# Filter spectra stored side by side and read by one transfer, with the end of the convolution stage reordered

## The chip, the cores and the metric

The kernel runs on one core of a Trainium2 chip. The metric is the device time of one execution in microseconds (us); before the change it is 2328.96 us, the median of three runs (2328.45 to 2333.43). The engines are named as in the profile: PE is the matrix engine (PEld its weight loads), DVE the vector engine, ACT the scalar engine, POOL is GpSimd, and SP is the engine that issues nearly all DMA transfers, in the order of its queue. A transfer is carried by the core's 16 DMA engines, which are shared by all queues.

## What is computed

One encoder block on 2048 positions of 1024 channels in float32. The input projection feeds a Fourier group (512 channels) and a gated long convolution of order two (512 channels); both are normalised, joined, projected out and followed by an MLP.

```python
h   = RMSNorm(x);  p = h @ W_in            # Fourier | x1 | x2 | v
y_f = RMSNorm_f(Re(FFT2(Fourier group)))   # 8 groups of 64 channels
z   = short_conv(v)
for n, gate in enumerate((x1, x2)):        # circular convolution of length 4096 by FFT
    y = irfft(rfft(z, n=2 * l) * rfft(k[n]))[:, :l]
    z = gate * (y + z * long_d[n])
y_h = RMSNorm_h(z)
x   = x + concat(y_f, y_h) @ W_out
x   = x + relu(RMSNorm(x) @ W_fc1)**2 @ W_fc2
out = RMSNorm_final(x)
```

## The kernel before

The program has six stages: input projection, the Fourier transform of the Fourier group beside the making of the filters, the long convolution, the output projection (`project_out`), and the two MLP products (`fc1`, `fc2`). The change touches the second, the third and the start of the fourth.

**Filters** (`filters`, line 471). There are eight units, one for each of two orders `n` and four groups of 128 channels `ct`. A unit generates its filter (`generate`, which needs decay tables `dec` that SP loads for two steps at a time), transforms it in a first stage (`stage1`, eight steps `c`) and a second stage (`stage2`, line 569, eight steps `q` of four matmuls). ACT copies each step's result from PSUM to the tile `ks`, and after every second step SP stores 128 rows of 4 KB to the scratch tensor `kd[ct][n]` in DRAM, named `spec` in the profile. The tile is [128, 32 frequencies, 128 channels]: partitions 0 to 63 hold the real parts and 64 to 127 the imaginary ones.

**Long convolution** (`hyena`, line 630). There are again eight blocks, four channel groups for each of two orders. A block transforms its signal (`first`, eight steps; the results `pz` are transposed by DVE into `G`), and then in eight steps `q` of `second` (line 669) makes four matmuls `pz`, multiplies them with the spectrum, and passes the product `y` on. The spectrum must be in both partition halves: `ks[:, 0]` has the real parts in all 128 partitions and `ks[:, 1]` the imaginary ones. `spectrum` (line 647) therefore issues two transfers of 256 KB for each step, one to partitions 0 to 63 and one to 64 to 127, from the same DRAM rows in pieces of 2 KB. The tile `ks` has four buffers: the load of step q+4 waits until step q has used its own. ACT makes the exchanged copy `zs`, DVE makes `y = pz * ks[:, 0]`, POOL makes `zs * ks[:, 1]`, and the sum is POOL's or DVE's. Three steps later (`LAG = 3`) `inverse` transforms `y` back (matmuls `pv`, copied by ACT into `V`), `turn` transposes `V` to `W` on DVE, and `gate` makes the last matmuls (`pb`) and multiplies with the gate `xg` into `zz`. The blocks overlap: in block i's steps the turns of block i-1, the gates of block i-2 and the first stage of block i+1 are interleaved. Behind the loop the last block's three remaining inverse steps, its turns and its gates are written out.

**Start of the output projection.** `Out.weights` (line 762) loads 128 rows of `w_out` (tile `ost`, which takes a buffer of `ks`) and splits them into a high part on ACT and a low part on DVE (line 185), in buffers of `G` and `V`. `Out.ahead` (line 796) takes the first two token tiles ahead: it loads and normalises their Fourier rows (`yf`), transposes them (`pt_y`), and makes their 48 matmuls with the first half of `w_out` (`po`). In the program these stand behind the last block's gates. `project_out` then normalises the tiles' convolution rows from `zz` (`ssq_h`, `v_h`, `oyn`), transposes them and adds the second half's matmuls.

What sets the order: every engine runs its own queue in order. A scheduler emits the program's instructions into these queues by its own estimate of when each is ready, so a row can stand earlier than the text has it. Buffers of the same tag are handed on in the order of allocation.

Of the kernel before, what the change touches and what calls it, by code (L numbers as in the profile page):

```python
# [10 lines left out]
F32 = mybir.dt.float32  # L11
# [116 lines left out]
P = 128  # L128
# [6 lines left out]
def hybrid_block(ctx: ExitStack, tc: tile.TileContext, A, out):  # L135
    nc = tc.nc
# [334 lines left out]
    def filters(ctx, fp, gp, zp, zzs, norms, emb, wo, e1k, f2):  # L471
# [9 lines left out]
        p = pa("plongd")  # L481
# [3 lines left out]
        class Unit:  # L485
# [83 lines left out]
            def stage2(self, q):  # L569
                p = pa("pk2")  # L570
                for j in range(4):
                    nc.tensor.matmul(p[:, 128 * j : 128 * j + 128], lhsT=f2[:, 4 * q + j, :], rhs=self.G[:, :, 4 * q + j], start=True, stop=True)
                if q % 2 == 0:
                    self.ks = sp.tile([P, 8, 128], F32, tag="ks", name="ks", bufs=3)
                nc.scalar.copy(self.ks[:, 4 * (q % 2) : 4 * (q % 2) + 4, :], p.rearrange("p (f c) -> p f c", f=4))
                if q % 2:
                    nc.sync.dma_start(kd[self.ct][self.n][:, 4 * q - 4 : 4 * q + 4, :], self.ks)

# [50 lines left out]

    def hyena(hp, wp, rp, zz, e1, b1, f2, a2, out_weights, out_ahead):  # L630

# [5 lines left out]
        class Block:  # L637
            def __init__(self, n, ct):
                self.n, self.ct = n, ct
                self.cs = slice(128 * ct, 128 * ct + 128)  # L640
                self.y, self.ahead = {}, None

# [4 lines left out]
            def spectrum(self, q):  # L647

                ks = hp.tile([P, 2, 4, 128], F32, tag="ks", name="ks", bufs=4)
                src = kd[self.ct][self.n][:, 4 * q : 4 * q + 4, :].rearrange("(s p) f c -> p s f c", s=2)  # L650
                for hf in (slice(0, 64), slice(64, 128)):
                    nc.sync.dma_start(ks[hf], src)
# [16 lines left out]
            def second(self, q):  # L669
                ks = self.ahead if q == 0 and self.ahead else self.spectrum(q)  # L670
                p = pa("pz2")
# [8 lines left out]
                nc.gpsimd.tensor_mul(zs, zs, ks[:, 1])  # L680
                (nc.gpsimd if self is not blocks[7] and q in (0, 1, 2, 3) else nc.vector).tensor_add(y, y, zs)
                self.y[q] = y
# [31 lines left out]
        for i in range(8):  # L714
            cur, old, older, new = (blocks[j] if 0 <= j < 8 else None for j in (i, i - 1, i - 2, i + 1))
            for q in range(8):
                if new and q == 7:
                    new.ahead = new.spectrum(0)
                cur.second(q)
# [35 lines left out]

    class Out:


        def __init__(self, wp, zp, zz, gy):
            self.wp, self.zp, self.zz, self.gy, self.w, self.begun = wp, zp, zz, gy, [], {}  # L760

        def weights(self, hp, k):
            if k % 2 == 0:
                n = "G" if k < 4 else "V"
                self.pair = self.wp.tile([P, 32, 128], F32, tag=n, name=n, bufs=2).bitcast(FR).rearrange("p (n f) c -> p n (f c)", n=4)
            t = hp.tile([P, 2, 4, 128], F32, tag="ks", name="ost", bufs=4).rearrange("p s f c -> p (s f c)")
            nc.sync.dma_start(t, A["w_out"][128 * k : 128 * k + 128, :])
            hi, lo = (self.pair[:, 2 * (k % 2) + j, :] for j in range(2))
            split(hi, lo, t, self.gy[:, k : k + 1])
            self.w.append((hi, lo))  # L770
# [44 lines left out]
    def project_out(op, work, rp, b):  # L815
# [67 lines left out]
        for i in range(NT + 1):  # L883
# [17 lines left out]
            else:  # L901
# [9 lines left out]
                for n, tag in (("m5", "G"), ("m6", "G"), ("m3", "V"), ("m7", "V")):  # L911
                    t = work.wp.tile([P, 32, 128], F32, tag=tag, name=f"b{n}", bufs=2).bitcast(FR).rearrange("p (n f) c -> p n (f c)", n=8)
                    b[n] = t[:, 0:4], t[:, 4:8]
# [418 lines left out]
    with pool("raws") as rp:  # L1332
        with pool("wts") as wp:
            work = Out(wp, zp, zz, gy)
            with pool("hyena") as hp:
                hyena(hp, wp, rp, zz, e1z, b1, f2, a2, work.weights, work.ahead)
            tabs.close()
# [63 lines left out]
```

## Time and profile before

| | |
|---|---|
| median of 3 runs | 2328.96 us (2328.45 to 2333.43) |
| profiled execution | 2339.88 us, of it 2336.8 us from the first to the last instruction (the span) |
| mean granted PE clock | 0.986 |
| PE busy | 2250.9 us, 96% of the span |
| PE weight loads | 1860.4 us, 80% |
| DVE, ACT, POOL busy | 65%, 47%, 36% |
| DMA | 468.42 MB, mean 200 GB/s |
| spectra stored (`spec<-ks`) | 32 transfers of 512 KB, issued from 484.7 to 637.5 us |
| spectra loaded (`ks<-spec`) | 128 transfers of 256 KB, issued from 638.0 to 840.2 us |

All times inside the program are microseconds from the span's start. A busy share is the part of a stretch in which an engine worked; the "DMA share" is the mean busy share of the 16 DMA engines. KB are 1024 bytes, MB and GB are powers of ten. In the timeline a row has start, duration, engine, line, operation, out<-in, count, and in brackets the idle time before it with what ended it.

### The profile page before, as it was taken

The page shows a single profiled execution, that of the slowest core. Times are in us where ns is not written, and L with a number is a line of the kernel's source. Part 1 is how long each engine was busy: PE and PEld are TensorE (multiplying, and loading weights), DVE is VectorE, ACT ScalarE, POOL GpSimd, SP SyncE. Part 2 cuts the span into 40 slices and gives each one's busy share as a digit, 9 for nine tenths or more (in the row PEclk, how much of TensorE's full clock was granted, in tenths as well). Part 3 has the DMA queues.
Part 4 walks back from the last instruction along what each step waited for, and adds up shares of the span by engine and source line. Part 5 has one row for each costly group of instructions (what it writes and reads, how often), then busy time and mean ns, then how long its engine had stood idle before and what let it go on. Part 6 is the DMA issues. An engine that isn't in the chain of part 4 may idle for free. (4 is left out here: it accounts for less than half of the span.)

```text
span 2336.8 us, 31028 instructions
## 1 busy us (share of the span) xinstructions
PE 2250.9 (96%) x11025; PEld 1860.4 (80%) x11025; DVE 1514.5 (65%) x2248; ACT 1106.6 (47%) x1826; POOL 840.6 (36%) x633
## 2 busy tenths in 40 slices
PE   7999998999899979998999999999999999999998
PEld 6887787799787858886788877888888888888886
DVE  6998666677577774547544457444466666866667
ACT  6554211466455554544555556555543333533334
POOL 3345322567465522215755556555400000000000
PEclk9999999999999989999999999999999999999999
DMA  7535888457688986567544456444479666866631
GB/s 250 181 137 176 290 308 321 144 199 233 214 201 188 200 218 189 177 182 237 161 150 152 152 204 208 152 150 149 149 279 373 234 191 198 284 207 193 198 117 72
DMA packets 294780, 468.42 MB, mean 200 GB/s; under 512 B 18453, under 2 KB 142687, under 8 KB 290273
## 3 DMA queue, kind: packets, MB, share of 16 engines
q1 hardware_dynamic: 291265, 460.43, 61.9%
q10 hardware_dynamic: 3360, 6.02, 0.8%
q8 instruction: 86, 1.41, 0.3%
q14 instruction: 69, 0.57, 0.1%
HBM read 312.54 MB, written 152.27 MB: 199 GB/s over the span
## 5 line engine op out<-in xcount | busy, mean ns | idle before, releaser
L181 ACT CAST qahm<-ra 128x1024 fp32r<-128x1024 f32 x110 | 116.0, 1054 | 345.8 <-PE p2u L190 172.0
L182 DVE TENSOR_TENSOR qalm<-ra,qahm 128x1024 fp32r<-128x1024 f32 x110 | 134.7, 1224 | 154.8 <-ACT qahm L181 151.7
L1183 POOL TENSOR_TENSOR acc<-acc,gfin 128x512 f32<-128x512 f32 x4 | 5.1, 1278 | 632.9 <-DMA out<-acc 625.4
L189 PE MATMUL pu<-wh,xh 128*128 128x512 f32 x512 | 206.4, 404 | 5.8 <-ACT wh L184 4.8
L190 PE MATMUL pu<-wl,xh 128*128 128x512 f32 x512 | 203.3, 397 | 5.9 <-DVE wl L182 3.7
L191 PE MATMUL pu<-wh,xl 128*128 128x512 f32 x512 | 203.2, 397 | 5.7 <-DVE xl L182 5.7
L190 PE MATMUL p2u<-qblm,qahm 128*128 128x512 f32 x504 | 196.2, 389 | 0.3 <-DVE qblm L182 0.3
L189 PE MATMUL p2u<-qbhm,qahm 128*128 128x512 f32 x504 | 195.9, 389 | 0.0
L191 PE MATMUL p2u<-qbhm,qalm 128*128 128x512 f32 x504 | 195.8, 389 | 0.0
L397 POOL TENSOR_TENSOR acc<-acc,cw 128x512 f32<-128x512 f32 x45 | 60.9, 1353 | 206.1 <-DVE acc L374 204.8
L182 DVE TENSOR_TENSOR qblm<-rb,qbhm 128x1024 fp32r<-128x1024 f32 x110 | 134.0, 1219 | 1.1 <-ACT qbhm L181 1.1
L181 ACT CAST ahm<-s 128x512 fp32r<-128x512 f32 x124 | 76.7, 621 | 94.0 <-PE p1v L190 54.1
L190 PEld LDWEIGHTS pu<-wl,xh 128*128 128x128 f32 x512 | 98.3, 192 | 28.7 <-DVE wl L182 4.1
L191 PEld LDWEIGHTS pu<-wh,xl 128*128 128x128 f32 x512 | 98.2, 192 | 28.3 <-DVE xl L182 7.7
L189 PEld LDWEIGHTS pu<-wh,xh 128*128 128x128 f32 x512 | 98.0, 192 | 27.8 <-ACT wh L184 6.2
L182 POOL TENSOR_TENSOR alm<-W,ahm 128x512 fp32r<-128x512 f32 x63 | 85.5, 1358 | 91.4 <-ACT ahm L181 91.4
L181 ACT CAST qbhm<-rb 128x1024 fp32r<-128x1024 f32 x110 | 115.3, 1048 | 4.6 <-DMA a1m<-c 2.8
L190 PEld LDWEIGHTS p2u<-qblm,qahm 128*128 128x128 f32 x504 | 94.6, 188 | 20.3 <-DVE qblm L182 0.8
L189 PEld LDWEIGHTS p2u<-qbhm,qahm 128*128 128x128 f32 x504 | 94.6, 188 | 20.2 <-issue 0.3
L191 PEld LDWEIGHTS p2u<-qbhm,qalm 128*128 128x128 f32 x504 | 94.6, 188 | 19.6
L181 ACT CAST ahm<-W 128x512 fp32r<-128x512 f32 x94 | 57.6, 615 | 103.4 <-PE p1u L190 100.8
L191 PE MATMUL p1u<-bm,alm 128*128 128x512 f32 x252 | 99.9, 396 | 6.4 <-DVE alm L182 6.4
(387 smaller groups left out, 6456.8 us busy)
## 6 DMA issues: line engine op xcount, KB each, us to landing
W<-in_w_fc SPq DMA_DIRECT2D x66, 512.0 KB, 4.6
ks<-spec SPq DMA_DIRECT2D x128, 256.0 KB, 6.8
rb<-td SPq DMA_DIRECT2D x64, 512.0 KB, 4.1
ra<-a1m SPq DMA_DIRECT2D x56, 512.0 KB, 6.0
ra<-a0m SPq DMA_DIRECT2D x54, 512.0 KB, 10.7
rb<-in_w_fc SPq DMA_DIRECT2D x46, 512.0 KB, 4.5
f<-in_w_fc SPq DMA_DIRECT2D x16, 1024.0 KB
td<-f SPq DMA_DIRECT2D x16, 1024.0 KB, 4.7
```

The source lines that it names most:

```text
L181: nc.scalar.copy(hi, src)
L182: (eng or nc.vector).tensor_sub(lo, src, hi)
L189: nc.tensor.matmul(o, lhsT=lh, rhs=rh, start=start, stop=False, skip_group_check=more)
L190: nc.tensor.matmul(o, lhsT=lh, rhs=rl, start=False, stop=False, skip_group_check=more)
L191: nc.tensor.matmul(o, lhsT=ll, rhs=rh, start=False, stop=stop, skip_group_check=more)
L397: nc.gpsimd.tensor_add(m1, m1, cw[:, 3, :])
L1183: nc.gpsimd.tensor_mul(acc[i][:, c], acc[i][:, c], gfin[:, c])
```

## The change

Three things are changed.

First, the spectrum's layout in DRAM is [64 partitions, 8 steps, 2 halves, 512] in place of [128, 32, 128], so that the real and the imaginary part of a step lie side by side. Each step of `stage2` has its own tile and stores it alone: 256 KB, whose DRAM side is walked half by half (2 x 64 rows of 2 KB). A step of `spectrum` is one load of 512 KB: its DRAM side is the same 64 rows of 4 KB taken twice (a leading dimension of 2 with stride 0), its SBUF side 128 partitions.

Second, in the last block the spectra of steps 2 to 7 are loaded at step 1; four of them go to a tile in `W`'s buffer. The loads of the first two token tiles' Fourier rows and of the first four pieces of `w_out` are issued at step 5, and the block's own gate load at step 6. Two of the block's sums move from DVE to POOL.

Third, the splits of the first four pieces of `w_out` and the 48 Fourier matmuls `po` stand ahead of the last block's turns and gates, and the buffers of the four pairs of pieces are G, V, G, V in place of G, G, V, V.

```diff
-    kd = [[scratch(f"spec{i}{n}", [P, 32, 128]) for n in range(2)] for i in range(4)]
+    kd = [[scratch(f"spec{i}{n}", [64, 8, 2, 512]) for n in range(2)] for i in range(4)]
...
-                if q % 2 == 0:
-                    self.ks = sp.tile([P, 8, 128], F32, tag="ks", name="ks", bufs=3)
-                nc.scalar.copy(self.ks[:, 4 * (q % 2) : 4 * (q % 2) + 4, :], p.rearrange("p (f c) -> p f c", f=4))
-                if q % 2:
-                    nc.sync.dma_start(kd[self.ct][self.n][:, 4 * q - 4 : 4 * q + 4, :], self.ks)
+                ks = sp.tile([P, 512], F32, tag="ks", name="ks", bufs=6)
+                nc.scalar.copy(ks, p)
+                nc.sync.dma_start(kd[self.ct][self.n].rearrange("p q s x -> s p q x")[:, :, q], ks)
...
-                ks = hp.tile([P, 2, 4, 128], F32, tag="ks", name="ks", bufs=4)
-                src = kd[self.ct][self.n][:, 4 * q : 4 * q + 4, :].rearrange("(s p) f c -> p s f c", s=2)
-                for hf in (slice(0, 64), slice(64, 128)):
-                    nc.sync.dma_start(ks[hf], src)
+                if self is blocks[7] and q > 3:
+                    if q == 4:
+                        self.room = rp.tile([P, 4, 2, 4, 128], F32, tag="W", name="ks4")
+                    ks = self.room[:, q - 4]
+                else:
+                    ks = hp.tile([P, 2, 4, 128], F32, tag="ks", name="ks", bufs=4)
+                src = kd[self.ct][self.n][:, q].rearrange("p s x -> p (s x)")
+                nc.sync.dma_start(ks.rearrange("p s f c -> p (s f c)"), src.unsqueeze(0).broadcast_to([2, 64, 1024]))
...
-                (nc.gpsimd if self is not blocks[7] and q in (0, 1, 2, 3) else nc.vector).tensor_add(y, y, zs)
+                (nc.gpsimd if q in ((0, 1) if self is blocks[7] else (0, 1, 2, 3)) else nc.vector).tensor_add(y, y, zs)
...
+                if i == 7:
+                    if q == 1:
+                        cur.ahead.update((k, cur.spectrum(k)) for k in range(2, 8))
+                    elif q == 5:
+                        ahead = work.ahead(hp)
+                        next(ahead)
+                        for k in range(4):
+                            work.load(hp, k)
+                    elif q == 6:
+                        cur.load()
...
-        old.load()
         for q in range(8 - LAG, 8):
             old.inverse(q)
-        ahead = out_ahead(hp)
-        next(ahead)
+        for k in range(0, 2):
+            work.weights(hp, k)
         for q in range(4):
             older.gate(q)
-            old.turn(2 * q)
-            old.turn(2 * q + 1)
+        for k in range(2, 4):
+            work.weights(hp, k)
+        next(ahead)
+        for c in range(8):
+            old.turn(c)
         next(ahead, None)
-        for k in range(0, 4):
-            out_weights(hp, k)
         for q in range(4):
             old.gate(q)
-        next(ahead, None)
         for k in range(4, 8):
-            out_weights(hp, k)
+            work.weights(hp, k)
```

The first place is SP's queue where the last two units' spectra are stored and the first block's loaded (`spec_65`, `spec_67` and so on are the tensors of single units; the sizes are those of the written side). Before:

```order
222 L577 DMA spec_63<-ks 128x1024 x2
223 L170 DMA a_5695<-in_a 128x4096
224 L577 DMA spec_63<-ks 128x1024
225 L170 DMA b_5697<-in_b 128x128
226 L577 DMA spec_65<-ks 128x1024 x4
227 L577 DMA spec_67<-ks 128x1024 x4
228 L652 DMA ks<-spec_60 64x2x512 x14
```

After:

```order
224 L576 DMA spec_63<-ks 2x64x512 x3
225 L171 DMA a_5759<-in_a 128x4096
226 L576 DMA spec_63<-ks 2x64x512 x2
227 L171 DMA b_5761<-in_b 128x128
228 L576 DMA spec_65<-ks 2x64x512 x8
229 L576 DMA spec_67<-ks 2x64x512 x8
230 L656 DMA ks<-spec_60 128x1x1024 x4
231 L644 DMA xg<-gates_58 128x16x128
```

There are twice as many stores of half the size, written as 2 x 64 rows, and half as many loads of twice the size; the stores still stand ahead of the first load in the same queue.

The second place is DVE's queue from the last block's last sum `y<-y,zs` to the norm of the first convolution rows (`v_h`). Before, from the end of the turns:

```order
956 L703 TENSOR_TENSOR zz<-pb,xg 128x4x128
957 L203 TENSOR_SCALAR nw_s<-nw_s,rc_s 128x1
958 L418 STREAM_TRANSPOSE W<-V 128x8x2x32 x2
959 L185 SCALAR_TENSOR_TENSOR G<-ost,gy,G 128x1024
960 L182 TENSOR_TENSOR yl<-pt_y,yh 128x512
961 L185 SCALAR_TENSOR_TENSOR G<-ost,gy,G 128x1024
962 L182 TENSOR_TENSOR yl<-pt_y,yh 128x512
963 L185 SCALAR_TENSOR_TENSOR G<-ost,gy,G 128x1024 x2
964 L703 TENSOR_TENSOR zz<-pb,xg 128x4x128 x4
965 L185 SCALAR_TENSOR_TENSOR V<-ost,gy,V 128x1024 x4
966 L216 TENSOR_SCALAR v_h<-ssq_h 128x1 x2
```

After:

```order
960 L685 TENSOR_TENSOR y<-y,zs 128x512
961 L186 SCALAR_TENSOR_TENSOR G<-ost,gy,G 128x1024 x2
962 L707 TENSOR_TENSOR zz<-pb,xg 128x4x128 x2
963 L186 SCALAR_TENSOR_TENSOR V<-ost,gy,V 128x1024
964 L707 TENSOR_TENSOR zz<-pb,xg 128x4x128 x2
965 L186 SCALAR_TENSOR_TENSOR V<-ost,gy,V 128x1024
966 L183 TENSOR_TENSOR yl<-pt_y,yh 128x512 x2
967 L419 STREAM_TRANSPOSE W<-V 128x8x2x32 x8
968 L186 SCALAR_TENSOR_TENSOR G<-ost,gy,G 128x1024 x2
969 L186 SCALAR_TENSOR_TENSOR V<-ost,gy,V 128x1024 x2
970 L707 TENSOR_TENSOR zz<-pb,xg 128x4x128 x4
971 L217 TENSOR_SCALAR v_h<-ssq_h 128x1 x2
```

The eight turns now stand behind four splits and the two `yl`, and all eight splits stand ahead of the last gates, where four stood behind them.

The third place is PE's queue at the same point. Before:

```order
2201 L673 MATMUL pz_7484<-G,f_2594 128x128 x4
2202 L689 MATMUL pv<-y,a_5695 128x128 x16
2203 L702 MATMUL pb<-G,b_5697 64x512 x8
2204 L785 MATMUL pt_y<-ident,yf 128x128 x4
2205 L785 MATMUL pt_y<-turn,yf 128x128 x4
2206 L702 MATMUL pb<-W,b_5697 64x512 x8
2207 L189 MATMUL po<-G,yh 128x512
```

After:

```order
2201 L677 MATMUL pz_7525<-G,f_2594 128x128 x4
2202 L693 MATMUL pv<-y,a_5759 128x128 x16
2203 L706 MATMUL pb<-G,b_5761 64x512 x8
2204 L803 MATMUL pt_y<-ident,yf 128x128 x4
2205 L803 MATMUL pt_y<-turn,yf 128x128 x4
2206 L190 MATMUL po<-G,yh 128x512
```

The 48 matmuls `po` start right behind the transposes, and the last gates `pb<-W` come behind them.

More of the change, by code (lines that the diff above doesn't have):

```diff
@@ L627, in filters, with hyena @@
                     units[j // 2].scale(2 * (j % 2) + 1, nc.vector)
-    def hyena(hp, wp, rp, zz, e1, b1, f2, a2, out_weights, out_ahead):
+    def hyena(hp, wp, rp, zz, e1, b1, f2, a2, work):
         def big(nm):
@@ L640, in __init__ @@
                 self.cs = slice(128 * ct, 128 * ct + 128)
-                self.y, self.ahead = {}, None
+                self.y, self.ahead = {}, {}
             def load(self):
@@ L669, in second @@
             def second(self, q):
-                ks = self.ahead if q == 0 and self.ahead else self.spectrum(q)
+                ks = self.ahead.pop(q) if q in self.ahead else self.spectrum(q)
                 p = pa("pz2")
@@ L717, in hyena @@
                 if new and q == 7:
-                    new.ahead = new.spectrum(0)
+                    new.ahead[0] = new.spectrum(0)
                 cur.second(q)
@@ L760, in __init__, with load @@
             self.wp, self.zp, self.zz, self.gy, self.w, self.begun = wp, zp, zz, gy, [], {}
+            self.raw = {}
+        def load(self, hp, k):
+            self.raw[k] = hp.tile([P, 2, 4, 128], F32, tag="ks", name="ost", bufs=4).rearrange("p s f c -> p (s f c)")
+            nc.sync.dma_start(self.raw[k], A["w_out"][128 * k : 128 * k + 128, :])
         def weights(self, hp, k):
+            if k not in self.raw:
+                self.load(hp, k)
             if k % 2 == 0:
-                n = "G" if k < 4 else "V"
+                n = "GVGV"[k // 2]
                 self.pair = self.wp.tile([P, 32, 128], F32, tag=n, name=n, bufs=2).bitcast(FR).rearrange("p (n f) c -> p n (f c)", n=4)
-            t = hp.tile([P, 2, 4, 128], F32, tag="ks", name="ost", bufs=4).rearrange("p s f c -> p (s f c)")
-            nc.sync.dma_start(t, A["w_out"][128 * k : 128 * k + 128, :])
             hi, lo = (self.pair[:, 2 * (k % 2) + j, :] for j in range(2))
-            split(hi, lo, t, self.gy[:, k : k + 1])
+            split(hi, lo, self.raw[k], self.gy[:, k : k + 1])
             self.w.append((hi, lo))
@@ L910, in project_out @@
                     split(*ahead[n], src)
-                for n, tag in (("m5", "G"), ("m6", "G"), ("m3", "V"), ("m7", "V")):
+                for n, tag in (("m5", "G"), ("m6", "V"), ("m3", "G"), ("m7", "V")):
                     t = work.wp.tile([P, 32, 128], F32, tag=tag, name=f"b{n}", bufs=2).bitcast(FR).rearrange("p (n f) c -> p n (f c)", n=8)
@@ L1335, in hybrid_block @@
             with pool("hyena") as hp:
-                hyena(hp, wp, rp, zz, e1z, b1, f2, a2, work.weights, work.ahead)
+                hyena(hp, wp, rp, zz, e1z, b1, f2, a2, work)
             tabs.close()
```

## The prediction

> **What bounds the kernel now.** I read the page first, then the busy times by stretch, the waits and the DMA issues of the two stretches in which spectra are stored and loaded, and last the timeline from the last spectrum to the first output matmuls.
>
> ```profile
> span 2336.8 us, 31028 instructions
> PE 2250.9 (96%) x11025; PEld 1860.4 (80%) x11025; DVE 1514.5 (65%) x2248; ACT 1106.6 (47%) x1826; POOL 840.6 (36%) x633
> ```
>
> Over the whole span PE is the bound: 86 us of 2336.8 are not matmul time. No edit here takes matmuls away, so a gain can only come out of that idle time. A loss has no such limit. The change rebuilds transfers, so the question is what the DMA engines do in the stretches that hold them.
>
> ```profile
> L577 SPq DMA_DIRECT2D spec<-ks x32: 319/320/1562, 484.7 to 637.5; - x32
> L652 SPq DMA_DIRECT2D ks<-spec x128: 573/605/4610, 638.0 to 840.2; - x128
> ```
>
> These are the issues of the two transfers on SP's queue, with count, issue durations in ns, and the time of the first and the last. I cut the program there: 484.7 to 641.2 us (stores), 641.2 to 850.3 us (loads, until the last one has landed), and 850.3 to 883.0 us (up to the first `po` of the convolution half). The last two rows below are stretches elsewhere with DMA at its limit.
>
> ```profile
> core 0: us, PE busy (x) PEld busy (x) DVE busy (x) ACT busy (x) POOL busy (x), PEclk, DMA share, GB/s
> 484.70:641.20 156.50, 146.93 (x1067) 133.46 (x1066) 106.84 (x185) 85.51 (x172) 99.82 (x83) 0.98 0.65 218
> 641.20:850.30 209.10, 193.54 (x1346) 168.39 (x1346) 154.28 (x239) 114.66 (x198) 120.35 (x107) 0.98 0.89 200
> 850.30:883.00 32.70, 26.95 (x109) 16.11 (x108) 24.68 (x49) 19.07 (x33) 5.24 (x5) 0.81 0.78 229
> 856.00:858.00 2.00, 2.00 (x12) 0.68 (x10) 1.70 (x3) 0.00 (x0) 0.00 (x0) 1.00 1.02 408
> 1740.00:1760.00 20.00, 20.00 (x90) 16.57 (x89) 16.18 (x16) 10.15 (x10) 0.00 (x0) 1.00 1.04 393
> ```
>
> Read the last two columns together. Between 641.2 and 850.3 us the 16 DMA engines are busy for 0.89 of the time, yet they move 200 GB/s: 200 / (16 x 0.89) = 14.0 GB/s per busy engine. In the two limit rows an engine moves 408 / 16 = 25.5 and 393 / 16 = 24.6 GB/s. So the half-partition loads, most of this stretch, are slow for each engine. There are 64 spectrum steps (eight blocks by eight), so a step takes 209.1 / 64 = 3.3 us, with 193.54 / 64 = 3.0 us of matmuls in it: DMA and PE are nearly level. What PE waits for there:
>
> ```profile
> engine line waited for: us in total, times, longest us
> PE pv L689 <- DVE y L681: 14.6, 14, 3.8
> ```
>
> The product `y` comes late because its spectrum does. 14.6 us is nearly all that faster loads could win there (15.6 us are idle).
>
> **How many engines carry a transfer.** This decides the case. Both new transfers have a DRAM side whose outermost dimension is 2: the store walks 2 halves by 64 rows of 2 KB, the load takes the same 64 rows of 4 KB twice. All old ones start with 64 or 128 rows. The page shows that this dimension can matter, in ACT's queue (packets, MB, share of 16 engines) and in the list of ACT's DMA issues:
>
> ```profile
> q10 hardware_dynamic: 3360, 6.02, 0.8%
> ...
> a1m<-c ACTq DMA_DIRECT2D x8, 256.0 KB, 2.3
> a1m<-s ACTq DMA_DIRECT2D x6, 256.0 KB, 4.8
> nb<-full ACTq DMA_DIRECT2D x6, 128.0 KB, 2.3
> nb<-full ACTq DMA_DIRECT2D x6, 126.0 KB
> out<-acc ACTq DMA_DIRECT2D x2, 256.0 KB
> a0m<-es ACTq DMA_DIRECT2D x1, 256.0 KB
> ```
>
> 17 transfers of 128 rows, 6 of 64 and 6 of 63 rows, each row 2 KB, are 2176 + 384 + 378 = 2938 packets, and 2938 x 2 KB is the 6.02 MB of the row. The other 422 packets carry next to no bytes; I read them as one closing packet for each engine of each transfer. With 16 engines always, 29 x 16 = 464 would be there. 422 is 23 x 16 + 6 x 9: the 63-row transfers ran on 9 engines, and 9 is the largest number up to 16 that divides 63. So a transfer is cut along its outermost dimension into equal parts, one for each engine. By the same reading an outermost 2 gives **two engines** to every new store and load. No transfer of before has so small an outer dimension, so this is an extrapolation; its other end is all 16 engines, rival A. I take the two engines, since the 63-row transfers are the only ones here whose row count 16 doesn't divide, and they follow it.
>
> The Trainium skill says the same in a rule that speaks against this change: in "DMA: Bandwidth & Descriptors", section "Why a DMA increments its semaphore by 16 and not by 1", the number of engines is the largest one up to 16 that divides the slowest dimension other than 1 of both sides, and the section "Rules for kernel authors" names a leading zero-stride broadcast of c copies as confined to at most c engines. By this rule the sum below stands; without it, rival A's would. The trace agrees for 63 rows (9 engines) and shows nothing for 2.
>
> **The sum.** The traffic of the two stretches and landing times (median us from issue), first the stores' stretch, then the loads':
>
> ```profile
> DMA packets 16216, 34.12 MB, mean 218 GB/s; under 512 B 942, under 2 KB 9262, under 8 KB 16075
> ...
> dec<-in_decay SPq DMA_DIRECT2D x20, 512.0 KB, 4.0
> spec<-ks SPq DMA_DIRECT2D x32, 512.0 KB, 3.7
> ```
>
> ```profile
> DMA packets 34614, 41.79 MB, mean 200 GB/s; under 512 B 2158, under 2 KB 18368, under 8 KB 34595
> ...
> ks<-spec SPq DMA_DIRECT2D x124, 256.0 KB, 6.9
> ```
>
> - Stores: 64 of 262,144 B by two engines at 24.6 GB/s each: 16.8 MB / 49.2 GB/s = 341 us.
> - Loads: 64 of 524,288 B at 25.5 GB/s each: 33.6 MB / 51 GB/s = 658 us, 10.3 us a step where it takes 3.3 now. Four buffers keep the queue full, so the two engines never run dry while PE waits. Matmuls (3.0 us a step) and everything of DVE and POOL lie beside it.
> - All other transfers of the two stretches still use 16 engines, the two busy ones among them, behind whatever is queued there: 34.12 + 41.79 - 16.8 - 33.6 = 25.5 MB, 1.6 MB for each engine, 63 us at 25.5 GB/s and 114 us at 14.0. I take 80, nearer to the first, since these are mostly whole-partition transfers.
> - Added waits: stores are issued twice as often, and the `dec` loads stand behind them in SP's queue. A `dec` load lands in 4.0 us now; behind six queued stores (six buffers, 5.3 us each) its part on the two engines comes some 30 us later. PE, ACT and DVE wait for the filter that it feeds. Mostly the two engines go on working meanwhile; where the stores are drained before the next filter is made they stand idle, once a unit for about one old landing, 4.0 us in five units: 20 us. Bounds: nothing, and 80.
>
> Together 341 + 658 + 80 + 20 = 1099 us in place of 156.5 + 209.1 = 365.6: **+733 us**.
>
> The rate has bounds too. Below 14.0 GB/s per busy engine nothing ran in these rows, above 25.5 nothing either. The 14.0 stems from 16 engines all writing into one partition half at a time; two engines do not get in each other's way there, so I take the limit rows' rate. The other end is rival C.
>
> **The tail (edits two and three).** Rows from the timeline (start, duration, engine, line, operation), and group rows of DVE from 640 to 890 us (count | busy us, mean ns):
>
> ```profile
> 851.62 0.69 DVE L681 TENSOR_TENSOR y<-y,zs 128x512 f32<-128x512 f32 x1 [0.65 <-POOL zs L680]
> ...
> 864.67 6.08 PE L702 MATMUL pb<-W,b 128*64 128x512 f32 x16
> ...
> 869.79 2.48 DVE L703 TENSOR_TENSOR zz<-pb,xg 128x512 f32<-128x512 f32 x4
> ...
> 870.68 0.50 PE L189 MATMUL po<-G,yh 128*128 128x512 f32 x1
> ...
> 872.19 3.75 DVE L185 SCALAR_TENSOR_TENSOR V<-ost,gy,V 128x1024 fp32r<-128x1024 f32 x3
> ...
> 877.56 0.21 DVE L216 TENSOR_SCALAR v_h<-ssq_h 128x1 f32<-128x1 f32 x2
> ...
> 881.48 0.39 PE L191 MATMUL po<-G,yl 128*128 128x512 f32 x1
> ...
> 882.98 0.50 PE L189 MATMUL po<-V,oyh 128*128 128x512 f32 x1 [0.24 <-ACT oyh L181]
> ```
>
> ```profile
> L703 DVE TENSOR_TENSOR zz<-pb,xg 128x512 f32<-128x512 f32 x32 | 21.8, 689 | 8.9 <-PE pb L702 8.9
> L185 DVE SCALAR_TENSOR_TENSOR G<-ost,gy,G 128x1024 fp32r<-128x1024 f32 x4 | 5.0, 1269 | 0.0
> L418 DVE STREAM_TRANSPOSE W<-V 128x512 f32<-128x512 f32 x56 | 36.1, 680 | 9.3 <-ACT V L690 9.1
> L182 DVE TENSOR_TENSOR yl<-pt_y,yh 128x512 fp32r<-128x512 f32 x2 | 1.4, 685 | 0.0
> ```
>
> The 48 `po` (870.68 to 881.87, 11 us of PE) move ahead of the gates `pb` and then lie beside DVE's turns; behind the gates only the norm is left. DVE becomes the chain. From the end of its last `y` (852.31) the new order gives it four splits (4 x 1.27 = 5.1), four `zz` (2.8), two `yl` (1.4), eight turns (5.4), four splits (5.1) and four `zz` (2.5): 22.3 us. From `v_h` to the first `po` on `oyh` it is 882.98 - 877.56 = 5.4 us as before. So the first convolution `po` is at 852.3 + 27.7 = 880.0 in place of 883.0: **-3 us**. What hides the loads of `w_out` and of `yf` here is that they are issued three steps earlier; if they come late, up to 3 us of this are lost. The two sums moved to DVE's neighbour and the removed buffer exchanges lie beside waits for spectra, so I cost them at nothing. Behind 883 us the program is the same.
>
> **Result of the sum.** The profiled execution took 2339.88 us: 2339.9 + 733 - 3 = 3070. It lies 10.9 us above the median of 2328.96, so the forecast is 3070 - 11 = 3059, said as **3060 us**.
>
> **The rivals.**
>
> *A, not slower: all 16 engines carry the new transfers.* Then the load fills 128 partitions at once. The limit rows, both of whole-partition transfers, give 408 GB/s against 200: a 512 KB load would take 1.3 us, below the 3.0 us of matmuls. Most of the 14.6 us of waits go, and the last block's `y` comes earlier; I keep 9 of them, because the turns of `G` and the POOL products stay, and 3 us of the tail: 2317 us. It decides as soon as a step's load lands within 3 us. For it speaks the 14.0 against 25.5 GB/s; against it the count of closing packets. Should the loads stay as slow as now on 16 engines, only the tail counts: 2326, within 0.2%, which is about what a measurement of this kernel can tell from no change.
>
> The Trainium skill's "SBUF — State Buffer", section "Door 1: The DMA port swizzle (why `[64,N]` ≈ `[32,N]`)", says that 64 partitions reach only half of the memory's ports. The trace agrees with its 14.0 GB/s per engine; by this rule alone the time would be rival A's.
>
> *B, only one of the two is confined.* Both have the 2 on the DRAM side only, the load as a reading side with stride 0 and the store as a writing side; one of them may be cut along the partitions instead. Loads alone: 658 + 30 of others - 209 = +479, less 3: 2805. Stores alone: 341 + 50 + 20 - 156.5 = +254, less rival A's 12: 2571.
>
> *C, two engines at the low rate.* At 14.0 GB/s each the loads take 33.6 MB / 28 GB/s = 1200 us, 542 more: 3600.
>
> **How the numbers follow.** Forecast 0.78; A 0.16 (0.13 faster, 0.03 within 0.2%); B 0.02 for each half; C 0.02. The forecast's own range is 2960 to 3380: downward no idle engines (-20), the others at 63 (-17) and a rate a tenth above the limit rows (-65 on the loads); upward a load rate half-way between 14.0 and 25.5 (+193), the others at 114 (+34) and 80 us of idle engines (+60), with some 30 for PE's clock in the waits. It holds most of its 0.78; to leave out no more than 2 in 10 the range takes in the loads-alone case and becomes **2780 to 3380**; A, the stores-alone case and C stay outside. Faster 0.13, same 0.03, slower 0.84.
>
> **What would show it.** Two engines: a `ks<-spec` load lands 30 to 41 us after its issue (three or four queued at 10.3) in place of 6.9; a store in tens of us in place of 3.7; the stretches' DMA share is below 0.25 and the rate near 50 to 70 GB/s; PE's waits become `pv` for `y` in nearly every step, some 7 us each, with the same matmul time. The tail: `po` before `pb<-W`, and some 28 us from the last `y` to the first `po` on `oyh`. The forecast is wrong if loads land within 10 us, if the DMA share in the loads' stretch stays above 0.5, or if one of the two stretches keeps its length.

## The result and the profile after

The changed kernel takes 3048.72 us (median of 4 runs, 3047.74 to 3052.54) against 2330.1 us before: ratio 1.3084, 95% interval 1.3053 to 1.3115. The forecast was 3060 us.

First the head of the page of the changed kernel, with the busy time of each engine:

```profile
span 3046.8 us, 31011 instructions
PE 2372.3 (78%) x11025; PEld 1953.1 (64%) x11025; DVE 1510.7 (50%) x2246; ACT 1106.2 (36%) x1826; POOL 842.7 (28%) x635
```

The work is the same, the matmuls number 11025 as before. The span has grown by 710 us, PE's busy time by only 121 (its mean granted clock is 0.883 in place of 0.986); the rest is time in which PE does nothing. Next the issues of the two new transfers (count, shortest, median and longest issue in ns, first and last time), and the stretches of the stores, of the loads, and of the tail, followed by two short stretches in which next to nothing but stores (810 us) or loads (1515 us) run:

```profile
L576 SPq DMA_DIRECT2D spec<-ks x64: 477/4786/11240, 477.3 to 848.4; - x64
L656 SPq DMA_DIRECT2D ks<-spec x64: 482/5743/21542, 853.5 to 1523.1; - x64
```

```profile
core 0: us, PE busy (x) PEld busy (x) DVE busy (x) ACT busy (x) POOL busy (x), PEclk, DMA share, GB/s
477.30:853.50 376.20, 204.66 (x1142) 176.37 (x1140) 104.40 (x191) 86.47 (x173) 100.51 (x84) 0.75 0.26 89
853.50:1559.80 706.30, 263.54 (x1284) 219.89 (x1284) 154.93 (x240) 120.41 (x209) 122.53 (x109) 0.66 0.19 64
1559.80:1587.00 27.20, 23.22 (x96) 13.94 (x96) 22.92 (x31) 9.57 (x13) 1.27 (x1) 0.87 0.25 84
...
810.00:840.00 30.00, 12.48 (x25) 7.08 (x25) 4.30 (x6) 3.52 (x6) 0.00 (x0) 0.50 0.13 51
1515.00:1535.00 20.00, 5.85 (x24) 5.26 (x24) 2.59 (x4) 3.50 (x5) 1.27 (x1) 0.59 0.13 52
```

The stores' stretch went from 156.5 to 376.2 us, the loads' from 209.1 to 706.3. In the short stretches the DMA share is 0.13, which is 2 engines of 16 (0.125), and they move 51 and 52 GB/s: 25.5 and 26 GB/s for each of two engines, what the limit rows of before had for each of sixteen. SP's issue of one transfer takes 4.8 and 5.7 us at the median where 0.3 and 0.6 us were enough before: I read this as a full queue at the two engines, with SP standing in the issue itself. What DVE waits for in the loads' stretch (853 to 1535 us; total, times, longest):

```profile
DVE y L683 <- DMA ks<-spec: 291.8, 40, 13.8
```

In 40 of the 61 steps of this stretch the product waits for its spectrum, 7.3 us each time. In the chain of work that ended last, transfers `ks<-spec` make up 74.6% of the time from 870 to 1560 us. In the stores' stretch (477 to 853 us) the filters wait for their `dec` loads, which stand behind the stores in SP's queue, as the prediction had it:

```profile
DVE kt L509 <- DMA dec<-in_decay: 148.0, 12, 17.3
```

One more row counts the engines directly. It is that of SP's queue (packets, MB, share of 16 engines), of the kernel before

```profile
q1 hardware_dynamic: 291265, 460.43, 61.9%
```

and of the changed kernel:

```profile
q1 hardware_dynamic: 284865, 460.42, 45.0%
```

Nearly the same bytes, 6400 packets fewer. Before, the stores had 32 x 128 rows of 4 KB and the loads 128 x 64 x 2 pieces of 2 KB, 20480 data packets, and, at one closing packet for each engine of each transfer, (32 + 128) x 16 = 2560 more. After, there are 64 x 128 pieces in the stores and 64 x 128 in the loads, 16384, and with two engines (64 + 64) x 2 = 256 closing packets. 23040 - 16640 = 6400, to the packet. With 16 engines the difference would have been 4608.

### The profile page after: what moved, and what is told of

It reads as the page before. It is cut to its first block, busy times and chain, and to the rows that moved or that the text cites. A ratio compares the mean times of both kernels' runs of the same rounds, so it can differ in the third digit from the quotient of the medians.

```text
span 3046.8 us, 31011 instructions
## 1 busy us (share of the span) xinstructions
PE 2372.3 (78%) x11025; PEld 1953.1 (64%) x11025; DVE 1510.7 (50%) x2246; ACT 1106.2 (36%) x1826; POOL 842.7 (28%) x635
## 4 chain that ended last, share of the span: by engine, by line
PE 53%; DMA 31%; DVE 5%; SPq 5%; ACT 3%; issue 2%; POOL 1%; ACTq 0%; DVEq 0%; POOLq 0%
DMA ks<-spec 17%; DMA dec<-in_decay 5%; PE p2u L191 4%; PE p2u L190 4%; PE p2u L192 4%; PE p1u L192 4%; PE p1u L190 3%; PE p1u L191 3%; SPq L656 3%; DMA spec<-ks 2%; PE pu L192 2%; PE pu L190 2%; PE pu L191 2%; PE p2v L191 2%; PE p2v L190 2%; PE p2v L192 2%
## 5 line engine op out<-in xcount | busy, mean ns | idle before, releaser
L693 PE MATMUL pv<-y,a 128*128 128x128 f32 x512 | 104.4, 369 | 304.7 <-ACT V L694 132.8
L693 PEld LDWEIGHTS pv<-y,a 128*128 128x128 f32 x512 | 91.7, 269 | 318.4 <-ACT V L694 134.3
L683 DVE TENSOR_TENSOR y<-pz,ks 128x512 f32<-128x512 f32 x64 | 43.8, 685 | 379.9 <-DMA ks<-spec 317.7
L191 PE MATMUL pu<-wl,xh 128*128 128x512 f32 x512 | 202.6, 396 | 6.3 <-DVE wl L183 3.7
L677 PE MATMUL pz<-G,f 128*128 128x128 f32 x512 | 95.4, 343 | 111.3 <-DVE G L419 49.1
L1201 POOL TENSOR_TENSOR acc<-acc,gfin 128x512 f32<-128x512 f32 x4 | 5.1, 1280 | 632.2 <-DMA out<-acc 625.0
L684 POOL TENSOR_TENSOR zs<-zs,ks 128x512 f32<-128x512 f32 x64 | 82.6, 1296 | 343.6 <-DMA ks<-spec 304.6
L677 PEld LDWEIGHTS pz<-G,f 128*128 128x128 f32 x512 | 89.8, 254 | 122.3 <-DVE G L419 51.5
L573 PE MATMUL pk<-Gk,f 128*128 128x128 f32 x512 | 79.9, 317 | 65.9 <-DVE Gk L419 60.6
L670 PE MATMUL pz<-zz,e1z 128*128 128x256 f32 x256 | 87.9, 489 | 52.9 <-ACT V L694 25.0
L573 PEld LDWEIGHTS pk<-Gk,f 128*128 128x128 f32 x512 | 76.0, 232 | 68.9 <-DVE Gk L419 62.0
L509 DVE TENSOR_TENSOR kt<-pk,dec 128x512 f32<-128x512 f32 x64 | 43.0, 679 | 153.5 <-DMA dec<-in_decay 148.0
```

The costliest lines, as they stand in the source:

```text
L191: nc.tensor.matmul(o, lhsT=lh, rhs=rl, start=False, stop=False, skip_group_check=more)
L670: nc.tensor.matmul(p[:, 256 * sp : 256 * sp + 256], lhsT=e1[:, sp, :], rhs=zz[:, :, lo : lo + 16], start=True, stop=True)
L683: nc.vector.tensor_mul(y, p3, ks[:, 0])
L693: nc.tensor.matmul(p[:, 128 * j : 128 * j + 128], lhsT=a2[:, 4 * q + j, :], rhs=self.y[q][:, j, :], start=True, stop=True)
```

## Experiments

The theory is that of the prediction: a transfer is cut along its outermost dimension, by the largest number up to 16 that divides it, so 2 halves mean two engines. The rivals are the layout, the number of stores, and the double read with stride 0.

**Both transfers cut by 64 rows** (layout and tail stay as changed):

```diff
-                nc.sync.dma_start(kd[self.ct][self.n].rearrange("p q s x -> s p q x")[:, :, q], ks)
+                for s in range(2):
+                    nc.sync.dma_start(kd[self.ct][self.n][:, q, s], ks[64 * s : 64 * s + 64])
...
-                nc.sync.dma_start(ks.rearrange("p s f c -> p (s f c)"), src.unsqueeze(0).broadcast_to([2, 64, 1024]))
+                for h in (0, 64):
+                    nc.sync.dma_start(ks[h : h + 64].rearrange("p s f c -> p (s f c)"), src)
```

> The changed kernel with one edit: each load of a spectrum step goes as two transfers of 64 rows (one for each partition half), each store as two of 64 rows. Layout, number of steps, order of the tail stay as changed. Theory 'outermost 2 means two engines': every transfer is cut along 64 rows again, 16 engines, so the whole loss goes: 2315 to 2330 us, a DMA share of 0.8 or more in the loads' stretch. Rival 'it is the layout': real and imaginary part side by side in DRAM, rows of 4 KB and twice as many stores ahead of the filters' loads in SP's queue: these are all still there, so the time stays above 2900 us.

Measured: 2350.15 us, ratio to before 1.0077 (1.0063 to 1.0091). 698.6 of the 718.6 us are gone with nothing changed but the cut (which also doubles the number of transfers), so the rival "layout" falls as the cause of the loss. The expectation itself was missed: 18 us stay, against the runs of the kernel before beside it (2332.55 us). The stretches of the stores and of the loads:

```profile
476.90:656.10 179.20, 155.86 (x1083) 140.98 (x1083) 108.07 (x188) 86.76 (x173) 100.70 (x84) 0.93 0.74 190
656.10:855.70 199.60, 189.91 (x1340) 164.77 (x1339) 153.42 (x236) 114.65 (x198) 124.17 (x110) 1.00 0.89 208
```

The loads' stretch is as good as it ever was. What is left over sits in the stores' stretch, 179.2 us here and 156.2 with the old stores in the kernel with the tail alone, below.

**Only the loads cut by 64 rows, and only the stores** (one of the two edits above each):

> The changed kernel with only the loads cut into two transfers of 64 rows; the stores stay as 2 x 64 rows. Theory 'two engines': the stores' part of the loss stays, some 240 us: 2560 to 2590 us; DMA share near 0.13 wherever only stores run. Rival 'only the load's double read with stride 0 is slow': 2315 to 2340 us.

> The changed kernel with only the stores cut into two transfers of 64 rows; the loads stay as one transfer with a leading 2 of stride 0. Theory 'two engines': the loads' part stays, 475 to 500 us: 2800 to 2830 us. Rival 'the stores are what holds everything up, the loads only come late behind them': below 2500 us.

Measured: 2557.59 us with the stores left on two engines, 2845.65 us with the loads left. Against the kernel with both cut, the stores cost 207.4 us and the loads 495.5, together 702.9, and both at once 698.6: the two losses add. Neither is an effect of the other, and stride 0 is not needed for it, since the stores have none. The first figure lies 2 us below its expected range. The second is 16 us above its own, which left out the 18 us that stay when the stores are cut into 128.

**Rows that 16 doesn't divide, in the kernel before.** This keeps the old layout, the old stores and whole rows, and has neither a leading 2 nor stride 0; only the rows of a half's load are split. Shown for 62 + 2; the others have 48 + 16 and 57 + 7.

```diff
-                for hf in (slice(0, 64), slice(64, 128)):
-                    nc.sync.dma_start(ks[hf], src)
+                for h in (0, 64):
+                    for r in (slice(0, 62), slice(62, 64)):
+                        nc.sync.dma_start(ks[h + r.start : h + r.stop], src[r])
```

> The kernel before the change with one edit: each half's load of 64 rows goes as 62 rows and 2 rows. No leading 2, no stride 0, the old layout, and whole rows as before. Theory 'the number of engines is the largest one up to 16 that divides the outermost dimension of both sides': 62 rows and 2 rows go by two engines each, so the loads take some 33.6 MB / 51 GB/s = 658 us: 2780 to 2830 us, DMA share near 0.13 where only these run. Rival 'stride 0 or the split of the DRAM side into halves is what is slow': as before plus some us for twice as many issues, 2328 to 2345 us.

> The control for the kernel with 62 and 2 rows: the same four loads for a step, but of 48 and 16 rows. 16 divides both, so by the theory all 16 engines carry them: 2328 to 2345 us, whatever the larger number of issues costs. Rival 'twice as many transfers are slow by themselves': as slow as the kernel with 62 and 2 rows.

> As the kernel with 62 and 2 rows, with 57 and 7 rows. By the theory 57 rows go by 3 engines (19 rows each) and 7 rows by 7 (one row each), so the busiest engines carry 20 of 64 rows where they carried 32: 33.6 MB x 20/64 / 26 GB/s = 403 us and some 45 of other traffic and waits, against 720 us measured with 62 rows and 277 with 48: 2560 to 2600 us. Rival 'any number of rows that 16 doesn't divide is slow in the same way': near 2845 us as with 62 rows.

Measured: 2845.51 us with 62 + 2 rows, 2596.07 with 57 + 7, 2409.57 with 48 + 16. The same four transfers a step, and only the row counts differ: against 48 + 16 rows, which 16 divides, 62 + 2 rows cost 435.9 us and 57 + 7 rows 186.5. The first figure is 16 us above its expected range, the second lies in it. A short stretch of loads with 62 + 2 rows:

```profile
1010.00:1020.00 10.00, 5.98 (x38) 5.62 (x37) 6.18 (x11) 3.09 (x6) 2.55 (x2) 0.83 0.14 52
```

and one with 57 + 7 rows:

```profile
1050.00:1060.00 10.00, 6.91 (x36) 6.75 (x37) 7.07 (x12) 3.56 (x6) 2.56 (x2) 0.62 0.21 77
```

52 GB/s are two engines at 26. With 57 + 7 rows the three busiest engines carry, by the theory, 20 of 64 rows each, so 77 GB/s are 77 x 20/64 = 24.1 for each of them. The closing packets say it exactly. SP's queue with 62 + 2 rows:

```profile
q1 hardware_dynamic: 289729, 460.42, 48.6%
```

with 57 + 7 rows:

```profile
q1 hardware_dynamic: 290497, 460.43, 53.6%
```

and with 48 + 16 rows:

```profile
q1 hardware_dynamic: 293313, 460.44, 60.1%
```

Before, the loads close with 128 x 16 = 2048 packets. With 62 + 2 rows it is 256 x 2 = 512, so 1536 fewer: 291265 - 1536 = 289729. With 57 + 7 rows it is 128 x (3 + 7) = 1280: 290497. With 48 + 16 rows 256 x 16 = 4096: 293313. All three to the packet. The kernel with both transfers cut by 64 rows fits as well: 16384 data and 256 x 16 closing packets are 2560 fewer than before, and its row has 288705. The theory stands at 62, 57, 7 and 2 rows. The Trainium skill's rule ("DMA: Bandwidth & Descriptors", section "Why a DMA increments its semaphore by 16 and not by 1") says the same, and these runs agree with it.

The control was dearer than expected, by 65 us: its loads' stretch is 281.2 us long, where that of the tail alone, below, with the old loads, is 202.6. The row:

```profile
640.00:921.20 281.20, 218.17 (x1355) 188.28 (x1354) 172.99 (x242) 114.22 (x198) 123.35 (x108) 0.91 0.71 150
```

The count of issues and the thinner transfers of 16 partitions were changed together here, so which of them costs it stays open. It is not mainly the landing of the spectra: POOL's waits for them are 26.3 us in that stretch, and no other engine has any.

**The parts alone.** The tail alone is the changed kernel with the old store and load lines and the old tensor; the layout alone is the kernel before with the side-by-side tensor and both transfers cut by 64 rows as above.

> Only the second and third part of the change (loads ahead in the last block, Fourier products and splits ahead of the last gates), with the spectra stored and loaded as before the change. Working of the prediction: 3 us less than before at the tail, 2324 to 2330 us. Rival 'the tail costs time, because the loads ahead collide with those of the last block': 2331 to 2340 us.

> Only the first part: side by side in DRAM, stores and loads of one step each, but cut as 64-row transfers; the order of the last block and the tail as before. If the row size of 4 KB in place of 2 KB matters for the loads into one half, the 14.6 us in which PE waits for y shrink: 2318 to 2328 us. If the loads are limited by writing into one half of the partitions, as 14.0 GB/s for each busy engine suggests, nothing changes: 2327 to 2333 us. Rival 'the layout itself costs': above 2340 us.

Measured: tail alone 2331.25 us, ratio 0.9995 (0.9987 to 1.0004), no difference that the runs could show, where 3 us less were expected. Layout alone 2346.92 us, ratio 1.0069 (1.0052 to 1.0086): its rival ("the layout itself costs") came true, and the remaining loss belongs to the first part of the change. The stretches of the tail alone:

```profile
478.80:635.00 156.20, 145.74 (x1051) 132.33 (x1051) 103.99 (x182) 85.44 (x171) 99.61 (x83) 0.97 0.63 213
635.00:837.60 202.60, 193.59 (x1363) 168.49 (x1362) 156.25 (x242) 114.76 (x199) 125.41 (x110) 1.00 0.92 207
```

and of the layout alone:

```profile
478.80:656.90 178.10, 154.48 (x1083) 139.17 (x1082) 108.16 (x188) 86.81 (x173) 100.82 (x84) 0.94 0.74 191
656.90:857.00 200.10, 189.73 (x1341) 164.85 (x1339) 154.55 (x238) 114.63 (x198) 120.49 (x108) 1.00 0.89 211
```

The stretch with 128 small stores is 22 us longer than that with 32 large ones; rows of 4 KB in place of 2 KB shorten the loads' by 2.5 us, hardly more than nothing. Of the 22 us, PE is busy for 8.7 and waits for 13.1 (23.6 in place of 10.5). Its largest wait has no counterpart with the tail alone:

```profile
PE pdk L544 <- DVE dk L533: 11.0, 4, 3.8
```

None of PE's waits in that stretch is for a transfer, DVE waits 0.9 us for `dec` and ACT 0.3 us for a store. So the small stores are hardly waited for themselves; the loss reaches PE through the work of the other engines on the filters, of which `dk` is a part. How the finer stores disturb that work is not shown.

**The stores on ACT's queue.** In the kernel with both cut, up to 14 stores stand in a row ahead of a unit's next `dec` load, where two stood before the change. I tried whether this place costs the 18 us, and the same move on the old stores with the new tail.

```diff
-                    nc.sync.dma_start(kd[self.ct][self.n][:, q, s], ks[64 * s : 64 * s + 64])
+                    nc.scalar.dma_start(kd[self.ct][self.n][:, q, s], ks[64 * s : 64 * s + 64])
```

> The kernel with both transfers cut by 64 rows, its 128 small stores issued on ACT's queue right behind the copy that fills the tile, in place of SP's. There the filters' dec loads no longer stand behind 14 stores that wait for their copies. If the 18 us of that kernel above the one before come from this place in SP's queue, they go: 2328 to 2337 us, and the stores' stretch is back near 156 us. Rival 'small stores of 128 KB are dear by themselves' (0.6 us of issue each, and the DMA share of 0.73 in place of 0.64): it stays at 2345 us or more.

> The kernel with the tail alone changed and the old spectra (32 stores of 512 KB), its stores issued on ACT's queue. Tried as a version that beats both: the dec loads are free of the stores, so the waits of PE in the stores' stretch (10 us before) may shrink: 2318 to 2330 us. Rival 'dec was early enough': 2328 to 2336 us, no different from the kernel with the tail alone.

Measured: 2362.16 us, ratio 1.0125 (1.0105 to 1.0144), and 2328.18 us, ratio 0.9991 (0.998 to 1.0002). The first guess falls: the loss does not go, it is 12 us more. The time is the rival's (2345 us or more), but that stores are dear by their number is not shown by it, since ACT's own order changed as well. The second is the fastest version of all, but its interval includes no difference, and it lies in the expected ranges of both the guess and its rival.

**Whole-partition loads on 16 engines.** Two forms of the prediction's rival A. First, the second half's load on ACT's queue, so that both halves can be written at once:

```diff
-                for h in (0, 64):
-                    nc.sync.dma_start(ks[h : h + 64].rearrange("p s f c -> p (s f c)"), src)
+                for h, eng in ((0, nc.sync), (64, nc.scalar)):
+                    eng.dma_start(ks[h : h + 64].rearrange("p s f c -> p (s f c)"), src)
```

> As the kernel with both kinds of transfer cut by 64 rows, but the load for partitions 64 to 127 is issued on ACT's queue in place of SP's, so that both halves can be written at once. If the low rate comes from one half being written at a time, the DMA engines move more than 14.0 GB/s each when busy, a step's loads land within 3 us, and the time is 2308 to 2322 us. If it has another cause, the time is within 3 us of the kernel with both halves on SP's queue; if ACT is held up by its loads' waits for free buffers, it is slower than that by up to 30 us.

Measured: 2360.54 us, ratio 1.0124 (1.0103 to 1.0145), 10 us slower than with both on SP's queue. The loads' stretch:

```profile
656.70:871.40 214.70, 194.89 (x1357) 170.32 (x1355) 161.73 (x249) 119.93 (x208) 124.27 (x110) 0.96 0.87 212
```

212 / (16 x 0.87) = 15.2 GB/s for each busy engine, against 208 / (16 x 0.89) = 14.6 with one queue. The loads land sooner (4.8 and 5.1 us at the median in place of 6.9), the engines are hardly faster, and the stretch is 15 us longer. The time fits the case that ACT is held up by its loads; which wait does it is not shown. Second, the spectra stored twice, with one load of 128 rows:

```diff
-    kd = [[scratch(f"spec{i}{n}", [64, 8, 2, 512]) for n in range(2)] for i in range(4)]
+    kd = [[scratch(f"spec{i}{n}", [128, 8, 2, 512]) for n in range(2)] for i in range(4)]
...
+                for s in range(2):
+                    nc.sync.dma_start(kd[self.ct][self.n].rearrange("(h p) q s x -> p h q s x", h=2)[:, :, q, s], ks[64 * s : 64 * s + 64].unsqueeze(1).broadcast_to([64, 2, 512]))
...
+                nc.sync.dma_start(ks.rearrange("p s f c -> p (s f c)"), src)
```

> The changed kernel with the spectra stored twice in DRAM, once for each partition half, so that one load of 128 rows (of 4 KB) fills all partitions: outermost 128, 16 engines, no stride 0. Each store is two transfers of 64 rows that write each row twice; 33.6 MB are stored in place of 16.8. Prediction's rival A: whole-partition loads by 16 engines land within 3 us and run near 25.5 GB/s for each engine, so PE waits less for y than the 7.7 us of the kernel with both cut by 64 rows, and the loads' stretch comes down to 193 to 200 us; the doubled stores add about 30 us to theirs: 2360 to 2385 us. If the low rate of 14.0 GB/s isn't from the partition half: landing 5 us or more.

Measured: 2385.22 us, ratio 1.0229 (1.0204 to 1.0254). Its stretches, with a short one of loads and other bulk transfers, and the landing of its loads (KB each, median us):

```profile
479.00:701.80 222.80, 167.44 (x1101) 149.17 (x1100) 107.31 (x190) 89.68 (x176) 101.40 (x84) 0.87 0.72 219
701.80:896.90 195.10, 187.87 (x1326) 164.42 (x1325) 148.72 (x243) 120.19 (x208) 124.68 (x110) 0.98 0.76 241
720.00:724.00 4.00, 4.00 (x31) 3.87 (x31) 1.71 (x3) 2.67 (x5) 3.52 (x3) 0.95 0.95 357
```

```profile
ks<-spec SPq DMA_DIRECT2D x54, 512.0 KB, 3.6
```

A load of 512 KB to all partitions lands in 3.6 us where one of 256 KB to a half took 6.9; over the stretch a busy engine moves 241 / (16 x 0.76) = 19.8 GB/s, and 357 / (16 x 0.95) = 23.5 in the short one. So the low rate of 14.0 GB/s comes with half-partition loads carried by sixteen engines, though the size and the number of the loads changed together with that here; two engines that write into one half, as with 62 + 2 rows, reach 26 GB/s each. The gain is small, 195.1 us in place of 199.6, since PE's own matmuls fill 188 of them, and the doubled stores cost 44 us where 30 were expected. The loads land in 3.6 us and not within 3.

## Why the prediction was right

- **Number of engines.** It rested on 9 engines for 63 rows and was carried over to a 2. The closing packets, the DMA share of 0.13, and the runs with 62, 57 and 48 rows show it. That the 63-row transfers are the only ones whose row count 16 doesn't divide holds for ACT's queue alone: in SP's there are `feat` loads of 66 rows (four of 132 KB), which the prediction left unread.
- **Rate of an engine.** Taken from the limit rows as 24.6 GB/s for stores and 25.5 for loads; measured 25.5 and 26. The low 14.0 GB/s, kept as rival C, does not return, neither with a load to both halves nor with 62 + 2 rows, where two engines write into one half.
- **The two stretches.** Forecast 1099 us; measured 376.2 + 706.3 = 1082.5, 16.5 less. By the measured rates the stores are 16.8 MB / 51 GB/s = 329 us and the loads 33.6 MB / 52 GB/s = 645, 25 us less than the sum's 999; the other traffic and idle engines together then took 108 us where the sum had 100; how they divide is not shown. By the shares that rival B gives, the sum had 411 us for the stores' stretch and 688 for the loads'. The first came out 35 us shorter and the second 18 us longer, so a part of the agreement is luck: two misses of opposite sign.
- **The profiled execution.** 3048.56 us against the sum's 3070: 16.5 us from the stretches, 7.4 from a stretch that began at 477.3 in place of 484.7 us (hardly an effect of the change: with only the loads' rows split it begins anywhere from 478.7 to 483.7), and 3 the other way from the tail.
- **The two parts apart.** Rival B gave 2571 us for the stores alone and 2805 for the loads alone. Measured 2557.6 and 2845.7. In the second the stores are the 128 small ones, and their stretch is 179.3 us in place of 156.5, which no step of the prediction had.
- **The tail: wrong in its size.** Forecast 3 us less. In the changed kernel the last `y` ends at 1561.88 us and the first `po` on `oyh` starts at 1592.41:

```profile
1561.19 0.69 DVE L685 TENSOR_TENSOR y<-y,zs 128x512 f32<-128x512 f32 x1
...
1566.03 0.69 DVE L707 TENSOR_TENSOR zz<-pb,xg 128x512 f32<-128x512 f32 x1 [1.75 <-PE pb L706]
...
1582.61 3.66 PE L706 MATMUL pb<-W,b 128*64 128x512 f32 x16
...
1583.74 0.69 DVE L707 TENSOR_TENSOR zz<-pb,xg 128x512 f32<-128x512 f32 x1 [1.14 <-PE pb L706]
...
1586.93 0.20 DVE L217 TENSOR_SCALAR v_h<-ssq_h 128x1 f32<-128x1 f32 x2
...
1592.41 0.79 PE L190 MATMUL po<-G,oyh 128*128 128x512 f32 x1 [1.96 <-ACT oyh L182]
1593.00 0.63 PE L191 MATMUL po<-G,oyh 128*128 128x512 f32 x1
```

  30.5 us, where it was 30.7. From `v_h` on it is 5.5 us, forecast 5.4; up to `v_h` it is 25.1 and not 22.3. The step that failed is "DVE becomes the chain": PE is still in it. DVE's own pieces are a little shorter than summed, but its `zz` wait 4.2 us for PE's `pb`: 2.5 us for the gates of the block before, which PE starts only at 1564.00, behind the last `pv`, and 1.7 us for the last gates, which it reaches only at 1582.61, behind its 48 `po`. The sum had these waits at nothing. And PE, having waited just before, starts the convolution half at 0.63 us a matmul in place of 0.40. With the tail alone the same point is later yet:

```profile
836.91 0.69 DVE L688 TENSOR_TENSOR y<-y,zs 128x512 f32<-128x512 f32 x1
...
845.88 1.11 PE L806 MATMUL pt_y<-ident,yf 128*128 128x128 f32 x4 [3.40 <-ACT yf L823]
...
861.77 3.66 PE L709 MATMUL pb<-W,b 128*64 128x512 f32 x16
862.90 0.69 DVE L710 TENSOR_TENSOR zz<-pb,xg 128x512 f32<-128x512 f32 x1 [3.82 <-PE pb L709]
...
871.66 0.79 PE L190 MATMUL po<-G,oyh 128*128 128x512 f32 x1 [2.04 <-ACT oyh L182]
```

  34.1 us from 837.60 to 871.66: PE waits for the normalised Fourier rows (`yf`, from ACT) before it can transpose them, so the 48 `po` start late, the gates stand behind them, and DVE's splits are done 3.8 us before `zz` can start. What the move took from behind the gates it put in front of them.
- **What would show it.** In the loads' stretch the DMA share (0.19) and the rate (64 GB/s) came as said; in the stores' stretch they are 0.26 and 89, just above. The 7 us a step are DVE's waits. PE's are not in nearly every step: `pv` waits 32 times for `y`, 162.2 us in all, and 6 times for `V`, 132.8. The DMA rows give no landing time for the two-engine transfers, but the chain has some of their loads from the end of the issue to the landing (start, duration):

```profile
873.95 35.06 DMA ks<-spec
...
910.64 27.23 DMA ks<-spec
```

  Others stand there with 23.8 us, so the forecast of 30 to 41 is of the right size. "The same matmul time" was wrong: matmuls in the loads' stretch took 263.5 us in place of 193.5, at a granted clock of 0.66. It can have cost little, since PE was idle for 443 us of that stretch.
- **Rival A** would have been off as well. With 16 engines the changed kernel is at 2350 us by half loads and at 2385 by whole ones, not at 2317: PE's waits for `y` shrink, but the stores' stretch grows (179.2 and 222.8 us), and the tail gives nothing.

Open: why the stretch with 128 stores of 128 KB is 22 us longer than with 32 of 512 KB. SP's issue time (0.58 us each in place of 0.32, 75 us in all in place of 10), the finer tiles, and the different order of DVE in that stage changed together, and the move to ACT's queue told only that the place ahead of the `dec` loads is not the whole of it. PE's waits there speak for the order of the work and against the transfers themselves.

## What to carry to other kernels

Before a transfer is given a new outermost dimension, look at its size: the number of DMA engines follows it, and a "single load for both halves" with a leading 2 runs on two engines of sixteen. Two transfers with 64 rows outermost, each to its own half, were better than one elegant one. It is cheap to see: the DMA share of a stretch (0.13 for two engines) and the packet count of the queue show the number of engines without any timing.

## What was unexpected of the hardware

- A trace counts one closing packet for each engine of a transfer; with it the totals of SP's and ACT's queues come out to the packet for the changed kernel and for every experiment.
- One DMA engine reaches 25.5 to 26 GB/s when only two run, and by the theory 24.1 when three carry most of the load, about the same as when all sixteen do (24.6 to 25.5).
- When transfers queue up on two engines, an issue takes SP 5.7 us at the median in place of 0.6, and everything behind it in its queue waits for that.
- Loads to the two partition halves from two queues at once raised the rate of a busy engine only from 14.6 to 15.2 GB/s over the loads' stretch, though one transfer to all partitions raised it to 19.8.
